# The order of gate and branch tiles in the tail of a hybrid decoder layer

## The chip, the cores and the metric

The kernel runs on one core of a Trainium2 chip. The metric is the device time of one execution in microseconds (us); where several runs are shown, their median counts.

## The reference, cut to what matters

One layer is computed in float32 for 512 prompt tokens and 8 sample tokens. The normalised and modulated input `h` goes through one projection `w_in`, whose columns feed two recurrent branches, their gates, and two merge gates `ga` and `gb`:

```
mod = silu(c) @ w_mod + b_mod                 # six parts: shift, scale and gate, twice
u = h @ w_in                                  # qa, fa, ia, oga, xb, yb, ga, gb
o_a = rmsnorm(hgrn2(...)) * silu(oga)         # eight heads
o_b = rglru(...) * gelu(yb)
merged = sigmoid(ga) * (o_a @ w_branch_a) + sigmoid(gb) * (o_b @ w_branch_b)
x = x + g1 * (merged @ w_out)
h2 = rmsnorm(x) * (1 + sc2) + sh2
x = x + g2 * (square(relu(h2 @ w_ff1)) @ w_ff2)
y = rmsnorm(x)
```

The final states of the recurrences and of the convolution are outputs too.

## The kernel before, in words

**Tiling.** Activations lie transposed, 128 features on the partitions and T = 520 tokens along the free axis, as two halves of 260. Every factor of a large product is split into a rounded part and the rest (`hi`, `lo`), and `products` (L144) makes hi*hi, hi*lo and lo*hi of it. So one output tile of 128 features over an inner length of 1024 (`gemm`, L156) is 8 x 3 x 2 = 48 matmuls. Such a tile is the unit of work below: a gate tile, a branch tile, an output projection tile.

**Weights.** `weights`, `take_w` and `ready_w` (L85 to L142) hand them out in the order of the steps. A 512 KB tile of weights is loaded on SP's queue (`_load_w`, L97) into one of four staging buffers `wst`, LOADS = 3 ahead of the splitting; ACT writes `whi` (L112), DVE `wlo` (L115), AHEAD = 2 tiles before use, into one of two places. The rows of `w_mod` need no splitting: they go through the same four buffers and are read there by PE.

**Modulation.** `mod` (L438) is one modulation step: two row tiles of 512 KB, on each of which `mod_rows` (L410) issues four matmuls (two records each in the trace, so 16 a step, L413). Four steps make a part; ACT then copies its sums (L418), and `mod_cols` (L421, matmuls of L427) turns them within the next gemm. Four parts are left for the tail, so 16 steps. `mod_step` in `run` puts one after a tile.

**Order of the steps.** `run` (L1555) writes a list of steps, each with its weights, and then calls them. First come eight heads, with the RG-LRU columns between them. Heads are finished two at a time (`heads_prompt`, L636), so that the end of heads 6 and 7 lies under the gate tiles that follow. `head_prompt` (L707) ends with: transposes (L714), states (L720), outputs (L731 and L733, into `pt`), their mean square (L738) and scale (L743) on ACT, transposes back (L747), the product with the output gate on DVE (L749), and a store to DRAM on SP's queue (L750). `heads_sample_done` (L626, L632) and `heads_sample_out` (L752, L758) close the sample tokens.

Then comes the tail:

- eight gate tiles b (`gate`, L891: gemm on `h`, then a sigmoid on ACT, L175, into a slot of pool `ma`). After the fourth, at TAIL = 3, `end_recurrences` and `begin_tail` (L1829) stand;
- eight branch tiles b (`branch`, L897: gemm on `ob`, then DVE multiplies the gate by it, L899). `rg_out` (L859) stands after the second: PE transposes of the last states (L871), copies (L873) and stores on POOL's queue (L875);
- eight times a gate tile a (into a slot of pool `tail`) and a branch tile a (`merge`, L901: gemm on `oa`, product, sum of both branches, split of the result);
- `load_xT` (L917: the residual's input, transposes of L933), `shifts` (L939: two memsets of the new `h` on POOL, L945), `begin_strassen` (L1840), then eight output projection tiles, which read all eight merged tiles.

`begin_tail` closes the pools of the recurrences (`rg`, `hg`) and opens those of the tail on their memory; a tile there waits for the tiles that it lies over. `load_branches` (L879) loads `ob` (L883) and `oa` (L887) back from DRAM on POOL's queue through five slots `t`; ACT and DVE split them (L205, L206).

**What sets the order on an engine.** The framework's scheduler places the instructions of neighbouring steps among each other on every engine; each engine then runs its own list in order. The list of steps is thus close to PE's order, but not the same. Only the beginning of the kernel (`begin`, L1635) is kept in order by hand; its instructions are recorded through a helper and show as L69. It ends with `again`, which puts the first modulation's shift into `h` (ACT into the rounded part, DVE through `ht` into the rest), with the pools `rg` and `hg` and with POOL's memsets of `fkq` and `at` (L1810). The first head's f, q and g products are made there; its v product (in `pt` and `pb`) is the first gemm behind.

Of the kernel before, what the change touches and what calls it, by code (L numbers as in the profile page):

```python
# [6 lines left out]
F32 = mybir.dt.float32  # L7
# [11 lines left out]
T = L + NB  # L19
HALF = T // 2  # L20
KO = D // 128
# [3 lines left out]
DFF = 4 * D  # L25
EPS = 1e-6
AHEAD = 2
TAIL = 3
URGENT = 200
TOGETHER = 400  # L30
NWM = 8
# [45 lines left out]
class Kernel:  # L77
# [1477 lines left out]
    def run(self):  # L1555
        tc, i, enter = self.tc, self.i, self.ctx.enter_context
        self.consts = enter(tc.tile_pool(name="consts", bufs=1))
        self.dram = enter(tc.tile_pool(name="dram", bufs=1, space=DRAM))
        self.sm = enter(tc.tile_pool(name="sm", bufs=2))
        self.wst = enter(tc.tile_pool(name="wst", bufs=WST))  # L1560
        self.ma = enter(tc.tile_pool(name="ma", bufs=8))
        self.ppt = enter(tc.tile_pool(name="ppt", bufs=1, space=PSUM))
        self.ppb = enter(tc.tile_pool(name="ppb", bufs=1, space=PSUM))
        self.pmm = enter(tc.tile_pool(name="pmm", bufs=2, space=PSUM))
        self.pps = enter(tc.tile_pool(name="pps", bufs=2, space=PSUM))
        self.whl = enter(tc.tile_pool(name="whl", bufs=2))
        self.act = enter(tc.tile_pool(name="act", bufs=2))
        self.early = ExitStack()
        self.hc = self.early.enter_context(tc.tile_pool(name="hc", bufs=1))
        self.ogs = self.hc.tile([128, H, NB], F32, name="ogs")  # L1570
        self.os = self.hc.tile([128, H, NB], F32, name="os")
        self.xlast = self.hc.tile([128, KO, 11], F32, name="xlast")
        self.hlast = self.hc.tile([128, KO, 9], F32, name="hlast")
        self.oaT_d = self.dram.tile([H, 128, L], F32, name="oaT_d")
        self.obT_d = self.dram.tile([KO, 128, T], F32, name="obT_d")
        self.oa, self.ob, self.merged = [], [], []

        win = i["w_in"][0]
        steps = []
        one = lambda name, m, fn, *a: steps.append(([(i[name][0], 0, m * 128)], fn, *a))  # L1580
        mods = [(p, k) for p in (2, 4, 3, 5) for k in range(0, KO, 2)]

        def mod_step():
            p, k = mods.pop(0)
            steps.append(([self.mod_key(p, k + n) for n in range(2)], self.mod, p, k))

        ga, gb = {}, {}
        self.rg = {}

        for h in range(H):  # L1590
            kf, kq, kv, kg = self.head_cols(h)
            steps.append(([kf, kq, kg, kv][FIRSTS if h == 0 else 0:], self.head_start if h == 0 else self.head, h))
            for n in (h - 1, h) if h % 2 else (h, h + 1):
                one("w_in", (40 if h % 2 else 32) + n, self.rg_y if h % 2 else self.rg_x, n)
        for m in range(KO):
            one("w_in", 56 + m, lambda m: gb.update({m: self.gate(7, m, self.slot(self.ma, "ma"))}), m)
            if m == TAIL:
                steps.append(([], self.end_recurrences))
                steps.append(([], self.begin_tail))
            if m > TAIL and m % 2:  # L1600
                mod_step()
        for m in range(KO):
            if m == 2:
                steps.append(([], self.rg_out))
            one("w_branch_b", m, lambda m: self.branch("w_branch_b", m, self.ob, gb[m]), m)
            if m <= TAIL or m % 2:
                mod_step()
        for m in range(KO):
            one("w_in", 48 + m, lambda m: ga.update({m: self.gate(6, m, self.slot(self.tail, "t"))}), m)
            one("w_branch_a", m, lambda m: self.merge(m, ga.pop(m), gb.pop(m)), m)  # L1610
            mod_step()
        steps.append(([], self.load_xT))
        steps.append(([], self.shifts))
        steps.append(([], self.begin_strassen))
        for m in range(KO):
            one("w_out", m, self.out_proj, m)
        steps.append(([], self.norm2))
        self.entries, self.use = self.plan()
        steps.append((self.entries[:FIRST], self.mlp))

        keys = [k for st in steps for k in st[0]]
        self.mlp_at = len(keys) - FIRST
        self.weights(keys)
        self.begin()
        for _, fn, *a in steps:
            fn(*a)
# [8 lines left out]
    def begin(self):  # L1635
# [167 lines left out]
        self.rgp = self.open_pool("rg", 2, reuse_waits="tile")  # L1803
        self.hg = self.scope.enter_context(self.tc.tile_pool(name="hg", bufs=2, reuse_waits="tile"))
        self.opened = {}
        self.X = [self.hg.tile([128, 3, T], F32, name=f"X{n}", bufs=1) for n in range(4)]
        self.fkq = [self.hg.tile([128, 3, 32], F32, name=f"fkq{n}", bufs=1) for n in range(4)]
        self.at = self.hg.tile([128, 2, NC, C], F32, name="at", bufs=1)
        for t in (*self.fkq, self.at):
# [19 lines left out]
    def begin_tail(self):  # L1829
        self.close_pool()  # L1830
        tc = self.tc
        pool = lambda name, bufs, **kw: tc.tile_pool(name=name, bufs=bufs, reuse_waits="tile", **kw)
        self.misc = self.ctx.enter_context(pool("misc", 1, side="right"))
        self.right = ExitStack()
        self.abb = self.right.enter_context(pool("abb", 16, side="right"))
        self.tail = self.open_pool("tail", 2, reuse_waits="tile")
        self.ab = self.scope.enter_context(pool("ab", 16))
        self.load_branches()

    def begin_strassen(self):  # L1840
        self.right.close()
        self.sw = self.ctx.enter_context(self.tc.tile_pool(name="sw", bufs=2, side="right", reuse_waits="tile"))


# [32 lines left out]
```

## Time and profile before

| | |
|---|---|
| three runs | 1031.09, 1031.99, 1032.07 us; median 1031.99 |
| the profiled execution | 1030.22 us |
| its span, first to last instruction | 1028.4 us |
| mean granted TensorE clock | 0.995 |
| PE, DVE, ACT, POOL busy | 97%, 66%, 50%, 12% of the span |

A row of the timeline reads: start in us, duration in us, engine, line, operation, output<-inputs, shapes, how many in a row, and in brackets the idle time ahead of it with what ended it. A row of a group has, after the bar, busy us and the mean ns of one, then the idle time ahead. A row of the DMA issues has the count, the size of each, and the median us from issue to landing. PE's matmuls overlap, so the step from one start to the next counts, not the duration of one. Lines named Lnnn are those of the kernel before; of after, those above L1580 are a few lines further down.

### The profile page before, as it was taken

The page shows a single profiled execution, that of the slowest core. Times are in us where ns is not written, and L with a number is a line of the kernel's source. Part 1 is how long each engine was busy: PE and PEld are TensorE (multiplying, and loading weights), DVE is VectorE, ACT ScalarE, POOL GpSimd, SP SyncE. Part 2 cuts the span into 40 slices and gives each one's busy share as a digit, 9 for nine tenths or more (in the row PEclk, how much of TensorE's full clock was granted, in tenths as well). Part 3 has the DMA queues.
Part 4 walks back from the last instruction along what each step waited for, and adds up shares of the span by engine and source line. Part 5 has one row for each costly group of instructions (what it writes and reads, how often), then busy time and mean ns, then how long its engine had stood idle before and what let it go on. Part 6 is the DMA issues. An engine that isn't in the chain of part 4 may idle for free. (4 is left out here: it accounts for less than half of the span.)

```text
span 1028.4 us, 23561 instructions
## 1 busy us (share of the span) xinstructions
PE 997.9 (97%) x9756; PEld 965.4 (94%) x9756; DVE 678.3 (66%) x1428; ACT 513.9 (50%) x964; POOL 123.8 (12%) x229
## 2 busy tenths in 40 slices
PE   5999999999999999989999999999999999999997
PEld 2899899999999999969999999999999999999997
DVE  7785868687586858355233347677776776777685
ACT  4555644644564554342122235466556655656663
POOL 3210000000000001011000001011421231232150
PEclk9999999999999999999999999999999999999998
DMA  9663353444334445268555568322672484274242
GB/s 324 222 201 111 95 160 101 133 134 134 101 103 149 116 124 156 89 230 264 167 157 173 162 179 240 97 83 62 134 180 78 93 177 121 52 157 101 63 83 83
DMA packets 201822, 143.67 MB, mean 140 GB/s; under 512 B 6767, under 2 KB 189703, under 8 KB 201707
## 3 DMA queue, kind: packets, MB, share of 16 engines
q1 hardware_dynamic: 191090, 128.08, 41.5%
q0 software_dynamic: 10608, 14.05, 7.1%
q8 instruction: 76, 1.25, 0.5%
q14 instruction: 32, 0.25, 0.1%
q10 hardware_dynamic: 16, 0.03, 0.0%
HBM read 123.61 MB, written 11.26 MB: 131 GB/s over the span
## 5 line engine op out<-in xcount | busy, mean ns | idle before, releaser
L151 PE MATMUL mm<-h,whi 128*128 128x260 f32 (+1 forms) x2944 | 489.2, 285 | 0.0
L151 PEld LDWEIGHTS mm<-h,whi 128*128 128x128 f32 x2944 | 409.1, 188 | 4.5 <-ACT whi L112 3.3
L151 PE MATMUL mm<-h,wlo 128*128 128x260 f32 x1472 | 302.0, 284 | 0.0
L115 DVE TENSOR_TENSOR wlo<-wst,whi 128x1024 fp32r<-128x1024 f32 x164 | 200.1, 1221 | 124.8 <-ACT whi L112 123.2
L112 ACT CAST whi<-wst 128x1024 fp32r<-128x1024 f32 x164 | 171.8, 1049 | 214.5 <-PE mm L151 180.5
L151 PEld LDWEIGHTS mm<-h,wlo 128*128 128x128 f32 x1472 | 230.0, 189 | 0.4 <-issue 0.2
L151 PE MATMUL mm<-a,whi 128*128 128x260 f32 x512 | 84.3, 285 | 0.0
L151 PEld LDWEIGHTS mm<-a,whi 128*128 128x128 f32 x512 | 70.4, 188 | 2.5 <-issue 2.1
L151 PE MATMUL mm<-a,wlo 128*128 128x260 f32 x256 | 52.3, 284 | 0.0
L883 POOL DMA_DIRECT2D t<-obT_d x8 | 4.4, 552 | 386.8 <-PE pb L788 311.5
L1276 DVE TENSOR_TENSOR f<-f 128x260 f32<-128x260 f32 x64 | 27.3, 427 | 27.6 <-ACT f L1271 26.9
L1265 ACT ACTIVATE ft<-ft,fsh 128x512 f32<-128x512 f32 (+2 forms) x36 | 24.0, 675 | 36.1 <-DVE ft L1262 36.1
L151 PE MATMUL mm<-b,whi 128*128 128x260 f32 x256 | 41.1, 282 | 0.0
L1268 POOL TENSOR_TENSOR ft<-ft,fsh 128x8 f32<-128x8 f32 x28 | 18.5, 659 | 186.7 <-DVE ft L1262 146.5
L151 PEld LDWEIGHTS mm<-a,wlo 128*128 128x128 f32 x256 | 39.6, 188 | 0.0
L151 PEld LDWEIGHTS mm<-b,whi 128*128 128x128 f32 x256 | 35.0, 188 | 0.0
L1310 POOL DMA_DIRECT2D ma<-snap x28 | 27.7, 1002 | 35.0 <-issue 26.2
L681 DVE TENSOR_TENSOR X<-X,tb 128x512 f32<-128x512 f32 x48 | 31.8, 682 | 0.0
L1292 POOL DMA_DIRECT2D ma<-snap x28 | 25.9, 927 | 41.1 <-DMA ma<-snap 29.3
L1271 ACT ACTIVATE f<-ft 128x520 f32<-128x520 f32 (+1 forms) x36 | 20.8, 587 | 15.1 <-POOL ft L1269 13.0
L597 DVE SCALAR_TENSOR_TENSOR st<-vb,fkq,st 128x128 f32<-128x128 f32 x64 | 17.5, 345 | 14.6 <-DMA vb<-vd 14.6
L151 PE MATMUL mm<-b,wlo 128*128 128x260 f32 x128 | 25.9, 284 | 0.0
(571 smaller groups left out, 1871.3 us busy)
## 6 DMA issues: line engine op xcount, KB each, us to landing
wst<-in_w_in_dram SPq DMA_DIRECT2D x64, 512.0 KB, 4.2
wst<-in_w_mod_dram SPq DMA_DIRECT2D x32, 512.0 KB, 4.6
wst<-in_w_ff_dram SPq DMA_DIRECT2D x64, 256.0 KB, 3.6
wst<-in_w_ff_dram SPq DMA_DIRECT2D x32, 512.0 KB, 4.9
wm<-in_w_mod_dram SPq DMA_DIRECT2D x16, 512.0 KB, 10.5
st<-in_state_hgrn_dram SPq DMA_DIRECT2D x8, 512.0 KB, 5.2
vb<-vd SPq DMA_DIRECT2D x8, 512.0 KB, 3.4
out_dram<-st SPq DMA_DIRECT2D x8, 512.0 KB
```

The lines of the kernel that those rows point to most:

```text
L112: ins = self.nc.scalar.copy(hi, st)
L115: self.nc.vector.tensor_tensor(lo, st, hi.bitcast(F32), OP.subtract)
L151: self.last_product = self.nc.tensor.matmul(ps[s][:, :c.stop - c.start], x, y[:, c], start=first and n == 0, stop=last and n == 2)
L597: nc.vector.scalar_tensor_tensor(st[:, b], vb[:, b], fkq[:, 1, b:b + 1], st[:, b], OP.mult, OP.add)
L681: nc.vector.tensor_tensor(half, half, fac, OP.mult)
L883: nc.gpsimd.dma_start(t, self.obT_d[n])
L1265: nc.scalar.activation(t[:, :p], t[:, :p], AF.Relu, bias=sh[:, 0:1])
L1268: eng.tensor_tensor(t[:, p:], t[:, p:], sh[:, 1:9], OP.add)
L1271: nc.scalar.activation(f, self.two(self.ft)[:, a:a + n], AF.Square)
L1276: self.nc.vector.tensor_tensor(f[:, n], f[:, a], f[:, b], op)
L1292: nc.gpsimd.dma_start(x[1][:, b], v[:, :n], accum_op=OP.add)
L1310: nc.gpsimd.dma_start(x[t][:, a], s[p], accum_op=OP.add)
```

## The change

All eight gate tiles b and then all eight gate tiles a come first; branch b's eight tiles follow, then branch a's eight. TAIL goes from 3 to 6, so `begin_tail` stands after the seventh gate tile b. Gate a's results get a pool `gp` of eight tiles on the right side of the memory, where `misc` was; `misc` is opened in `begin_strassen` only, when `gp` and `abb` are closed. The 16 modulation steps are spread evenly over the 25 tiles behind `begin_tail`. Of the four tiles `X`, the first two move to a pool `hx` of their own, above `hg`.

```diff
-TAIL = 3
+TAIL = 6
...
-        def mod_step():
+        def mod_step(due):
+            if due < 0.999 or not mods:
+                return due
             p, k = mods.pop(0)
             steps.append(([self.mod_key(p, k + n) for n in range(2)], self.mod, p, k))
+            return due - 1
...
-        for m in range(KO):
-            one("w_in", 56 + m, lambda m: gb.update({m: self.gate(7, m, self.slot(self.ma, "ma"))}), m)
-            if m == TAIL:
+        tiles = [("b", m) for m in range(KO)] + [("a", m) for m in range(KO)]
+        share, due = len(mods) / (2 * len(tiles) - TAIL - 1), 0.0
+        for g, m in tiles:
+            if g == "b":
+                one("w_in", 56 + m, lambda m: gb.update({m: self.gate(7, m, self.slot(self.ma, "ma"))}), m)
+            else:
+                one("w_in", 48 + m, lambda m: ga.update({m: self.gate(6, m, self.slot(self.gp, "gp"))}), m)
+            if (g, m) == ("b", TAIL):
                 steps.append(([], self.end_recurrences))
                 steps.append(([], self.begin_tail))
-            if m > TAIL and m % 2:
-                mod_step()
-        for m in range(KO):
-            if m == 2:
+            if (g, m) > ("b", TAIL) or g == "a":
+                due = mod_step(due + share)
+        for g, m in tiles:
+            if (g, m) == ("b", 2):
                 steps.append(([], self.rg_out))
-            one("w_branch_b", m, lambda m: self.branch("w_branch_b", m, self.ob, gb[m]), m)
-            if m <= TAIL or m % 2:
-                mod_step()
-        for m in range(KO):
-            one("w_in", 48 + m, lambda m: ga.update({m: self.gate(6, m, self.slot(self.tail, "t"))}), m)
-            one("w_branch_a", m, lambda m: self.merge(m, ga.pop(m), gb.pop(m)), m)
-            mod_step()
+            if g == "b":
+                one("w_branch_b", m, lambda m: self.branch("w_branch_b", m, self.ob, gb[m]), m)
+            else:
+                one("w_branch_a", m, lambda m: self.merge(m, ga.pop(m), gb.pop(m)), m)
+            due = mod_step(due + share)
+        assert not mods, mods
...
-        self.X = [self.hg.tile([128, 3, T], F32, name=f"X{n}", bufs=1) for n in range(4)]
+        hx = self.scope.enter_context(self.tc.tile_pool(name="hx", bufs=1, reuse_waits="tile"))
+        self.X = [(self.hg if n > 1 else hx).tile([128, 3, T], F32, name=f"X{n}", bufs=1) for n in range(4)]
...
-        self.misc = self.ctx.enter_context(pool("misc", 1, side="right"))
         self.right = ExitStack()
+        self.gp = self.right.enter_context(pool("gp", 8, side="right"))
         self.abb = self.right.enter_context(pool("abb", 16, side="right"))
...
     def begin_strassen(self):
         self.right.close()
+        self.misc = self.ctx.enter_context(self.tc.tile_pool(name="misc", bufs=1, side="right", reuse_waits="tile"))
         self.sw = self.ctx.enter_context(self.tc.tile_pool(name="sw", bufs=2, side="right", reuse_waits="tile"))
```

## The prediction

> **What bounds the kernel now.** I read the page's busy times first, then the table of 20 us stretches, then PE's instructions in order of time in the one stretch that is not full, and last the queues that feed it.
>
> ```profile
> PE 997.9 (97%) x9756; PEld 965.4 (94%) x9756; DVE 678.3 (66%) x1428; ACT 513.9 (50%) x964; POOL 123.8 (12%) x229
> ```
>
> ```profile
> 420.00:440.00 20.00, 20.00 (x171) 20.00 (x170) 6.13 (x12) 7.14 (x19) 0.00 (x0) 1.00 0.39 122
> 440.00:460.00 20.00, 15.24 (x120) 10.31 (x119) 11.90 (x41) 7.68 (x16) 4.33 (x8) 0.91 0.64 216
> 460.00:480.00 20.00, 20.00 (x184) 18.40 (x183) 13.77 (x23) 7.80 (x12) 3.70 (x7) 1.00 0.88 279
> 480.00:500.00 20.00, 20.00 (x181) 18.55 (x180) 5.78 (x6) 3.15 (x3) 0.52 (x1) 1.00 0.67 200
> ```
>
> PE is the bound: 97% of the span, and full before and after the seam between recurrences and tail. Columns of the stretches: length, then busy us of PE, PEld, DVE, ACT and POOL, granted clock, DMA share, GB/s. The change can only win what PE loses at the seam, 440 to 460: 4.76 us idle, and a granted clock of 0.91.
>
> ```profile
> 438.08 0.49 PE L151 MATMUL mm<-h,whi 128*128 128x260 f32 x2
> ...
> 441.29 0.40 PE L151 MATMUL mm<-h,wlo 128*128 128x260 f32 x2
> 443.42 0.66 PE L747 MATMUL pt<-ident,g 128*128 128x128 f32 x4 [1.73 <-ACT g L743]
> 444.86 0.65 PE L632 MATMUL pt<-ident,sev 128*128 128x128 f32 x4 [0.79 <-DVE e L749]
> 445.78 3.48 PE L413 MATMUL pt<-wst,cT 128*32 128x256 f32 x30 [0.27 <-DVE os L634]
> 449.18 0.43 PE L758 MATMUL ps<-sq,ones_r 128*128 128x64 f32 x2
> 449.55 0.62 PE L413 MATMUL pt<-wst,cT 128*32 128x256 f32 x2
> ...
> 456.06 0.62 PE L413 MATMUL pt<-wst,cT 128*32 128x256 f32 x2 [1.98 <-DMA wst<-in_w_mod_dram]
> ...
> 470.65 0.60 PE L871 MATMUL ps<-ident,hlast 128*9 128x128 f32 x4
> 471.00 0.36 PE L151 MATMUL mm<-a,wlo 128*128 128x260 f32 x1
> ...
> 474.52 0.53 PE L427 MATMUL pb<-ident,modev 128*128 128x36 f32 x4
> 474.98 1.07 PE L413 MATMUL pt<-wst,cT 128*32 128x256 f32 x16
> ...
> 481.93 1.07 PE L413 MATMUL pt<-wst,cT 128*32 128x256 f32 x16
> ...
> 494.62 1.07 PE L413 MATMUL pt<-wst,cT 128*32 128x256 f32 x16
> ```
>
> ```profile
> 444.00:446.00 2.00, 0.95 (x9) 0.62 (x12) 0.87 (x2) 0.24 (x2) 0.00 (x0) 0.89 0.16 63
> 446.00:448.00 2.00, 2.00 (x24) 0.88 (x19) 1.44 (x3) 2.00 (x5) 0.45 (x1) 0.50 0.22 78
> ```
>
> At 441.53 (two matmuls after 441.29, at 0.12 each) the last gate tile is done. Everything left needs either the end of head 7 (L747, L632) or branch b's operand, which comes after it. PE does the modulation rows it has (L413) at a granted clock down to 0.50, starts branch b, and waits 1.98 for the next rows.
>
> ```profile
> 436.49 0.33 SPq L101 DMA_DIRECT2D wst<-in_w_mod_dram  x1
> 444.83 0.33 SPq L750 DMA_DIRECT2D oaT_d<-e  x1
> 446.92 0.38 SPq L103 DMA_DIRECT2D wst<-in_w_branch_b_dram  x1
> 447.77 0.82 SPq L101 DMA_DIRECT2D wst<-in_w_mod_dram  x1
> ...
> 447.56 1.76 POOL L883 DMA_DIRECT2D t<-obT_d  x3 [52.59 <-DVE a L206]
> ```
>
> SP's own order makes it worse: the store of head 7's result (L750) stands ahead of branch b's weights, so nothing was issued on it for 8 us, and then weights, rows and branch operands are fetched at once.
>
> **The change, part by part.** The built program of after, compared engine by engine, has the same instructions as before on every engine; only places between some 441 and 630 us differ, and some waits.
>
> (1) *Gates first.* How much does the seam cost? From 441.53 to the sixth modulation step at 481.93 are 40.40 us. In them PE does four branch tiles of 48 matmuls, five modulation steps, 24 transposes, one L427 and one L758. A tile with a step is 481.93 - 474.98 = 6.95; two tiles with a step are 494.62 - 481.93 = 12.69; so a tile is 5.74 and a step 1.21. Four transposes are 471.00 - 470.65 = 0.35, so 24 are 2.1; L427 is 474.98 - 474.52 = 0.46; L758 is 449.55 - 449.18 = 0.37. Work: 4 x 6.95 + 1.21 + 2.1 + 0.46 + 0.37 = 31.94. **Lost at the seam: 40.40 - 31.94 = 8.46 us**: the idle 4.76, the rest slow clock and refilled pipeline.
>
> ```profile
> L112 ACT CAST whi<-wst 128x1024 fp32r<-128x1024 f32 x164 | 171.8, 1049 | 214.5 <-PE mm L151 180.5
> ...
> wst<-in_w_mod_dram SPq DMA_DIRECT2D x32, 512.0 KB, 4.6
> ```
>
> ```profile
> t<-oaT_d POOLq DMA_DIRECT2D x8, 256.0 KB, 6.7
> t<-obT_d POOLq DMA_DIRECT2D x3, 260.0 KB, 8.0
> ```
>
> In after, eight gate tiles a, which need only h, stand at that place. On PE's list, behind head 7's last state product (ahead of 438.08), come 69 gate matmuls, L747, 27 more, L632, 22 more, the first rows and L758, then gates to the end. At 0.12 us a matmul (5.74 / 48) L747 is reached at 438.08 + 8.3 = 446.4. In before its operand was there at 443.42; ACT now has one weight copy ahead of it (L112, 1.05 us by its group), which makes 444.5. So no wait. Branch b starts some 50 us later (eight gates at 5.74 and steps), when its operands have long been split: in before they were all there within the first branch tile. All 8.46 can go.
>
> What is late next? Rows and weights. The four staging buffers go round in turn: a step's second row tile is issued when the step before has read its first, and is needed one tile and one step later, 5.74 + 1.21 = 6.95 us. The median landing of the 32 is 4.6. In the crowded seam rows issued at 447.77 were there at 456.06: 8.3 us, 1.3 too many. After has 11 loads of branch operands (8 x 256 and 3 x 260 KB, which took 6.7 and 8.0 us to land between 430 and 500) beside its first two or three steps, as before had. The leftover is bounded by nothing and two waits like 456.06's (2 x 1.98 = 4.0). I take 0.4, nearest to nothing: before ran 460 to 480 at a DMA share of 0.88 with PE full.
>
> A rule that speaks against this part: the Trainium skill ("DMA: Bandwidth & Descriptors", Queues, rings and completion order) says that each DMA engine serves the queues with work in turn, packet by packet. By it SP's weights would get half while POOL's loads run: no trace here shows the split, and the sum by it would be about 2 us worse, one such wait.
>
> (2) *Modulation steps spread evenly.* 16 steps as before, on 25 places. Eight of the 15 distances are one tile long, in before two. They cost nothing while rows land within 6.95 us; the price if not is a rival below.
>
> (3) *Pool gp, TAIL 6, rg_out, shifts.* Gate a's sigmoid writes gp, which lies over X0 and X1 (last used by heads 4 and 5): its only wait in the built program is PE's. Eight results held until the merge cost no engine time. POOL's two memsets of h (L945) move ahead of the state outputs (L875) and wait for the last gate, which PE has done before L871: nothing queues. The merge of the last branch a (three operations of DVE and one of ACT, on half L112's columns, so under 4 x 1.05 = 4.2 us) is hidden by the first seven eighths of an output projection tile, 7/8 x 5.74 = 5.0; without that cover it costs 4.2 at most. ACT and DVE have room: under 14 of 20 us busy from 440 to 500. misc, opened later, is first written when the last merge has read gp.
>
> (4) *X0 and X1 in pool hx.* This moves addresses at the head of the kernel, which the diff does not show. In before POOL's memsets (L1810) had nothing to wait for; in after they wait for the last ht on DVE.
>
> ```profile
> 53.07 0.54 DVE L69 TENSOR_SCALAR ht<-xn,modT,shp 128x512 f32<-128x512 f32 x1
> ...
> 53.98 0.68 DVE L69 TENSOR_TENSOR h<-ht,h 128x512 fp32r<-128x512 f32 x1
> 54.59 1.79 DVE L69 TENSOR_SCALAR ht<-xn,modT,shp 128x512 f32<-128x512 f32 x1
> ...
> 53.74 0.99 POOL L1673 TENSOR_TENSOR h<-fs,h 128x8 fp32r<-128x8 f32 x1
> 54.67 0.53 POOL L1810 MEMSET fkq<- 128x96 f32 x4
> 55.13 0.96 POOL L1810 MEMSET at<- 128x1024 f32 x1
> ...
> 57.88 0.28 PE L151 MATMUL pb<-h,whi 128*128 128x260 f32 x1
> 58.16 0.39 PE L151 MATMUL pt<-h,whi 128*128 128x260 f32 x1
> ...
> 58.86 0.28 PE L151 MATMUL pb<-h,whi 128*128 128x260 f32 x1
> 59.41 0.39 PE L151 MATMUL pt<-h,whi 128*128 128x260 f32 x1 [0.28 <-DVE h L69]
> ```
>
> Beside the memsets one ht took 1.79 instead of 0.54, 1.25 more, and PE then stood 0.16 and 0.43 us over its 0.12 at 58.16 and 59.41. Without that delay both stalls go: **0.6**. At worst the memsets, later now, hit the last subtraction in its place, and the gain is 0; DVE's subtraction at 53.98 beside a POOL operation took its usual 0.68, so I take 0.6. The Trainium skill ("SBUF — State Buffer", Who interferes with whom) says that a two-input DVE operation collides with GpSimd reads, not with pure writes: by it too 0.6. The read at 53.74 did not slow 53.98 either, which the rule would have had. The first sigmoid into X0 waits for PE's last shift product instead of for DVE's last ht, which comes later, so it holds up nobody.
>
> **Sum.** 8.46 - 0.4 + 0.6 = 8.66 us. On the profiled execution, 1030.22 (span 1028.4 and 1.8 around it), that is 1021.6; the median of the runs shown is 1031.99, 1.77 above, so **1023.4 us** predicted. The bounds: at best 9.1 (1022.9), at worst 8.46 - 4.0 = 4.5 (1027.5).
>
> **The rivals.** (A) *The seam's DMA crowd stays*, chance 0.15: POOL's operand loads now run beside gates that need weights as well, and rows come late once or twice. For it: 8.3 us against 6.95. Against it: SP now has weights up to gate a 3 issued ahead of head 7's store, and the loads have eight tiles' time instead of one. The rule above (the Trainium skill, "DMA: Bandwidth & Descriptors") would lead here. Gain 5 to 6.5: 1025.5 to 1027.
>
> (B) *The even spread starves PE*, slower, 0.04: in all eight short distances the second row tile lands after 8.3 us instead of 4.6. Each costs 1.35, together 10.8, against a gain of 8.46: 2.3 slower, 1034.3. It decides from 8.46 / 8 = 1.06 us each, a landing of 8.0. Against it: outside the seam DMA's share of 480 to 500 is 0.67, and before had such a distance from 474.98 to 481.93 with PE full.
>
> (C) *Nothing comes of it*, 0.03: the seam's slack is given back where something else is timed by DMA or by the chain of heads, so 1031.5. Against it: PE is full from 460 on.
>
> (D) The forecast with its 0.4 and 0.6, 0.78: 1022.3 to 1025.5 with the spread of runs.
>
> **How the numbers follow.** 1023.4 is D's. D and nearly all of A hold the time 9 in 10; cutting A's top, the range for 8 in 10 is 1022.3 to 1026.6. Faster than 0.2% (2.1 us, about what a measurement tells from no change) are D and A: 0.93; C makes 0.03 the same; B 0.04 slower.
>
> **What would show it.** Right: 440 to 460 with PE at 20.00 and clock 1.00; no wait at L747 and L632; the ht by 54.59 at 0.54; the whole span from the first rows to the first L933 shorter by some 8. Wrong: waits of PE for row tiles behind gates a 2 and a 3 (A), or at every second tile up to the output projection (B); a new wait of PE near 120 or 200 us (C).

## The result, and the profile after

After: **1024.07 us**, median of four runs (1022.04 to 1024.82); before beside it 1031.54 (1029.1 to 1032.07). The ratio is 0.9929, with a 95% interval of 0.9907 to 0.9951, so the change gains 0.7%: 7.5 us between the medians, and by the interval 5.1 to 9.6. The profiled execution of after is the slowest of its four, 1024.82 us with a span of 1023.0.

The page's busy times of after, then its stretches of 20 us (length, busy us of PE, PEld, DVE, ACT and POOL with their instructions, granted clock, DMA share, GB/s):

```profile
PE 998.3 (98%) x9756; PEld 969.0 (95%) x9756; DVE 676.8 (66%) x1428; ACT 512.7 (50%) x964; POOL 123.6 (12%) x229
```

```profile
420.00:440.00 20.00, 20.00 (x171) 20.00 (x170) 7.66 (x14) 6.24 (x11) 0.00 (x0) 1.00 0.31 96
440.00:460.00 20.00, 20.00 (x174) 18.97 (x173) 10.97 (x31) 10.57 (x26) 3.25 (x6) 1.00 0.49 146
460.00:480.00 20.00, 20.00 (x181) 18.56 (x180) 12.64 (x30) 10.07 (x16) 2.69 (x5) 1.00 0.97 328
480.00:500.00 20.00, 20.00 (x182) 18.65 (x181) 3.89 (x5) 4.91 (x7) 0.23 (x2) 1.00 0.63 186
```

PE's busy time is what it was; the span is shorter. In 440 to 460, PE has gone from 15.24 busy at a clock of 0.91 to 20.00 at 1.00. The DMAs are most crowded in 460 to 480, as in before (0.97 against 0.88), and PE stays full beside them.

PE's timeline of after at the seam, and SP's queue there. A bracket at the end of a row would be idle time ahead of it; PE's rows have none:

```profile
440.43 0.39 PE L733 MATMUL pt<-g,X 128*128 128x128 f32 x2
...
448.92 0.60 PE L747 MATMUL pt<-ident,g 128*128 128x128 f32 x4
...
452.60 0.60 PE L632 MATMUL pt<-ident,sev 128*128 128x128 f32 x4
...
455.78 0.64 PE L413 MATMUL pt<-wst,cT 128*32 128x256 f32 x8
456.35 0.43 PE L758 MATMUL ps<-sq,ones_r 128*128 128x64 f32 x2
```

```profile
439.00 7.69 SPq L103 DMA_DIRECT2D wst<-in_w_in_dram  x2
450.28 0.34 SPq L750 DMA_DIRECT2D oaT_d<-e  x1
452.50 4.30 SPq L101 DMA_DIRECT2D wst<-in_w_mod_dram  x2
```

In before, PE came to the end of head 7 (L747, L632) with nothing else to do, and then read 30 records' worth of rows in one lump. Here the gates' matmuls stand between these rows, the first lump of rows is 8, and SP has issued two weight tiles of the gates (L103) ahead of the store L750, where before had one row tile.

To see where the time came from, I cut each profiled execution at four instructions of PE: the first v product (the first gemm, L151), the last L733 (the end of head 7 begins), the first L933 (behind the tail), the end. In us:

| | start of the span to v product | to the last L733 | **tail**: to the first L933 | to the end | span |
|---|---|---|---|---|---|
| before | 53.45 | 384.60 | **172.90** | 417.49 | 1028.43 |
| after | 56.30 | 384.24 | **165.01** | 417.49 | 1023.04 |

The tail gained 7.89. The last stretch is the same to a hundredth. At the start, which the change doesn't touch, this execution of after lost 2.85, beside a lower granted clock. These are the 20 to 40 us of before and then of after:

```profile
20.00:40.00 20.00, 18.30 (x180) 14.68 (x179) 14.16 (x33) 10.15 (x16) 0.87 (x3) 1.00 0.97 336
```

```profile
20.00:40.00 20.00, 18.56 (x145) 15.86 (x146) 13.16 (x27) 10.14 (x16) 0.87 (x3) 0.83 0.94 327
```

The clock was 0.83 instead of 1.00, and PE did 145 matmuls instead of 180 in those 20 us. The starts of all 14 profiled kernels go by this clock and not by kernel: eight at 1.00 took 53.42 to 53.69, two at 0.91 took 53.92 and 54.02, four at 0.83 took 55.46 to 56.30. One execution of 1024.82 therefore says little by itself, and the experiments below are compared by the tail. The tail repeats well: e8 and e12, the same kernel, both took 164.76.

### The profile page after: what moved, and what is told of

Read it like the earlier page. It is cut to its first block, busy times and chain, and to the rows that moved or that the text cites. A ratio compares the mean times of both kernels' runs of the same rounds, so it can differ in the third digit from the quotient of the medians.

```text
span 1023.0 us, 23553 instructions
## 1 busy us (share of the span) xinstructions
PE 998.3 (98%) x9756; PEld 969.0 (95%) x9756; DVE 676.8 (66%) x1428; ACT 512.7 (50%) x964; POOL 123.6 (12%) x229
## 5 line engine op out<-in xcount | busy, mean ns | idle before, releaser
L151 PE MATMUL mm<-h,whi 128*128 128x260 f32 (+1 forms) x2944 | 490.4, 286 | 0.0
L151 PEld LDWEIGHTS mm<-h,whi 128*128 128x128 f32 x2944 | 410.2, 189 | 3.3 <-issue 1.8
L151 PE MATMUL mm<-h,wlo 128*128 128x260 f32 x1472 | 302.9, 285 | 0.3 <-DVE wlo L115 0.3
L151 PEld LDWEIGHTS mm<-h,wlo 128*128 128x128 f32 x1472 | 230.9, 189 | 1.1 <-DVE wlo L115 0.5
L151 PE MATMUL mm<-a,whi 128*128 128x260 f32 x512 | 84.0, 284 | 0.0
L151 PEld LDWEIGHTS mm<-a,whi 128*128 128x128 f32 x512 | 70.3, 188 | 1.7 <-ACT whi L112 1.6
L151 PE MATMUL mm<-a,wlo 128*128 128x260 f32 x256 | 52.3, 284 | 0.0
L151 PE MATMUL mm<-b,whi 128*128 128x260 f32 x256 | 41.6, 285 | 0.0
L151 PEld LDWEIGHTS mm<-a,wlo 128*128 128x128 f32 x256 | 39.6, 188 | 0.0
L151 PEld LDWEIGHTS mm<-b,whi 128*128 128x128 f32 x256 | 35.1, 188 | 2.1 <-ACT whi L112 1.2
L151 PE MATMUL mm<-b,wlo 128*128 128x260 f32 x128 | 25.9, 283 | 0.0
```

The source lines that it names most:

```text
L151: self.last_product = self.nc.tensor.matmul(ps[s][:, :c.stop - c.start], x, y[:, c], start=first and n == 0, stop=last and n == 2)
```

## The experiments

Each experiment has one profiled execution, and one of them was timed in further runs as well. In the table, "idle" is PE's idle time in the tail, and "rest" runs from the last L733 to the end. The rest is needed for the three kernels with dense steps (e7, e9, e10): their last column transposes (four matmuls of L427 and eight transposes of L924) come before the first L933 instead of behind it, some 1.1 us that move from the last stretch into the tail. In the other kernels that last stretch took 417.38 to 418.24, so differences in the rest of under 0.9 us say little.

| | what it is | tail | rest | idle | that run |
|---|---|---|---|---|---|
| before | | 172.90 | 590.39 | 4.76 | 1030.22 |
| after | | 165.01 | 582.50 | 0.00 | 1024.82 |
| e1 | after, no gate a ahead of branch b | 172.46 | 590.63 | 3.62 | 1030.49 |
| e5 | after, one gate a ahead | 168.13 | 586.30 | 0.98 | 1024.95 |
| e6 | after, two gates a ahead | 166.05 | 583.78 | 0.04 | 1022.44 |
| e2 | before with pool hx | 172.83 | 591.08 | 3.51 | 1030.62 |
| e3 | after without pool hx | 165.12 | 582.51 | 0.00 | 1024.88 |
| e4 | before, head 7's store on POOL | 173.81 | 591.32 | 5.67 | 1030.50 |
| e7 | after, a step behind every tile | 175.13 | 591.42 | 4.33 | 1032.50 |
| e9 | e7, operand loads late | 170.52 | 586.90 | 2.60 | 1028.65 |
| e10 | a step behind every tile from gate a 2 | 165.85 | 582.21 | 0.00 | 1025.72 |
| e8 | after, steps behind branch tiles only | 164.76 | 582.60 | 0.00 | 1020.92 |
| e11 | after with TAIL = 3 | 171.93 | 589.61 | 4.01 | 1028.67 |
| e12 | e8 again, timed | 164.76 | 582.42 | 0.00 | 1022.64 |

### Is it the order of the tiles, and how many does it take? (e1, e5, e6)

Theory: PE lacks work at the seam, so the gain goes by the work put there. e1 is after with its eight gates a back in front of their branch tiles; e5 and e6 leave one or two of them ahead.

```diff
-        for g, m in tiles:                  # the gates
+        for g, m in tiles[:KO + N]:         # N = 0, 1, 2
...
             else:
+                if m >= N:
+                    one("w_in", 48 + m, lambda m: ga.update({m: self.gate(6, m, self.slot(self.gp, "gp"))}), m)
+                    due = mod_step(due + share)
                 one("w_branch_a", m, lambda m: self.merge(m, ga.pop(m), gb.pop(m)), m)
```

> After with everything but the order of the tiles: gate tiles a stand again in turn with branch tiles a, while TAIL 6, the even spread of the steps, pools gp and hx stay. 'The tail' is the time from head 7's last state product (last L733) to the first transposes of the residual's input (first L933): 172.90 us in before, 165.01 in after. Theory of the prediction (only gate tiles that need nothing of the heads cover the seam): the tail stays at 172 to 174, PE idles 4 to 6 us between 440 and 460, one execution about 1030 to 1032. Rival (the even spread of the steps and the later begin_tail made the gain): 165 to 167.

> After with only the first gate tile a ahead of branch b; the other seven stand each before its branch tile a, as before had all eight. The tail is the span from the last L733 to the first L933: 172.90 us before, 165.01 after, 172.46 with no gate tile a ahead. Theory (the gain is work that PE can do while head 7 ends and branch b's operands come, so it goes by the amount): one tile covers 48 x 0.12 = 5.74 us of the lost 8.46, so the tail is 165.0 + 2.7 = 167.7 (166.5 to 169). Rival (it's SP's order and the crowd of loads, so a single tile helps little, because branch b's weights still stand behind head 7's store): 170 to 172. Rival (any tile is enough): 165.

> After with two of the gate tiles a ahead of branch b, the other six as before. Theory (by the amount): two tiles are 11.5 us of work, more than the lost 8.46, so nothing is left to gain: tail 165.0 to 166. Rival (crowd of loads: rows and operands are fetched at once, and only eight tiles' time spreads them): two or three late rows of 1.3 to 2 us each, 168 to 171.

Measured: 172.46, 168.13 and 166.05, against 165.01 with eight. Above the seam's work of 172.90 - 8.46 = 164.44, that is 8.0, 3.7, 1.6 and 0.6 us. The first tile is worth 4.3 and the second 2.1; all of the other six together 1.0. The theory holds with its sizes, but for two small misses: e6 is 0.05 above its range, and e1's idle time was 3.62 where 4 to 6 was expected. "Any tile is enough" falls, as does "a single tile helps little". PE's waits at the seam in e1, and then in e5:

```profile
444.14 1.12 PE L747 MATMUL pt<-ident,g 128*128 128x128 f32 x4 [2.43 <-ACT g L743]
446.04 1.12 PE L632 MATMUL pt<-ident,sev 128*128 128x128 f32 x4 [0.79 <-DVE e L749]
447.42 1.93 PE L413 MATMUL pt<-wst,cT 128*32 128x256 f32 x16 [0.27 <-DVE os L634]
```

```profile
447.55 1.07 PE L413 MATMUL pt<-wst,cT 128*32 128x256 f32 x16 [0.27 <-DVE os L634]
...
467.64 0.74 PE L151 MATMUL mm<-a,whi 128*128 128x260 f32 x4 [0.71 <-ACT whi L112]
```

In e1 the waits of before are back, and behind them the slow clock: four transposes last 1.12 us instead of 0.60, and 16 records of L413 1.93 instead of 1.07. The idle 3.62 is under half of the 8.0 lost. Most of the rest is this clock: it averaged 0.51 from 444 to 451, which makes some 3.4 us (an estimate, 7 x 0.49). In e5 the waits for g and e are gone and the clock holds at 1.00. Only 0.98 of the 3.7 us that e5 still loses is idle time; the rest is in steps of PE that are longer than usual, most of them from 462 to 468, and was not taken apart.

### Does the placement of X0 and X1 do anything? (e2, e3)

e2 is before with pool hx and nothing else of the change; e3 is after without it.

```diff
+        hx = self.scope.enter_context(self.tc.tile_pool(name="hx", bufs=1, reuse_waits="tile"))
-        self.X = [self.hg.tile([128, 3, T], F32, name=f"X{n}", bufs=1) for n in range(4)]
+        self.X = [(self.hg if n > 1 else hx).tile([128, 3, T], F32, name=f"X{n}", bufs=1) for n in range(4)]
```

> Before with pool hx alone. Theory: only the head of the kernel changes. POOL's memsets wait for the last ht on DVE, the ht that took 1.79 us takes 0.54, PE's two short stalls in the first gemm go, and the stretch from the first gemm (first L151) to head 7's last state product (384.60 us in before, 384.24 in after) is 384.2; the tail stays at 172.9. Rival (the 0.4 of that stretch comes from elsewhere): 384.6.

> After with all four X back in pool hg, so that gp lies over other tiles of the recurrences. Theory (the order makes the gain, placement makes none): the tail is 165.0 within 0.5, the stretch ahead of it 384.6. Rival (gp has to lie over X0 and X1): the first sigmoids of gate a wait for tiles that head 7 still uses, its store included, ACT stands and PE with it, and the tail is 167 or more.

The long stretch to the last L733 can't tell: 384.34 and 385.02, where after had 384.24 and before 384.60, and the other experiments between 382.86 and 386.25. Its first part can. From the v product to the first L632, the three kernels without hx (before, e3, e4) took 134.59, 134.54 and 134.56. Seven with hx (e1, e2, e5, e6, e8, e11, e12) took 133.74 to 133.76. That is **0.8 us**, to a few hundredths in every kernel. Compared matmul by matmul from the v product on, e12 is ahead of before by 0.25 at the 40th and by 0.79 at the 46th, and that difference stays, within 0.05, to the 1200th: it arises just where before's two stalls lay. (The other four kernels with hx, after among them, took 135.27 or 135.28. They lost 1.5 us further on, at a slow clock; see the end.) DVE, POOL and PE of e2 there:

```profile
54.57 0.54 DVE L69 TENSOR_SCALAR ht<-xn,modT,shp 128x512 f32<-128x512 f32 x1
...
58.35 0.53 DVE L587 COPY fkq<-ma 128x8 f32<-128x8 f32 x1
```

```profile
57.43 0.53 POOL L1811 MEMSET fkq<- 128x96 f32 x4 [2.72 <-DVE ht L69]
57.88 0.98 POOL L1811 MEMSET at<- 128x1024 f32 x1
```

```profile
57.98 0.28 PE L151 MATMUL pt<-h,whi 128*128 128x260 f32 x1
58.10 0.28 PE L151 MATMUL pb<-h,whi 128*128 128x260 f32 x1
58.22 0.28 PE L151 MATMUL pt<-h,wlo 128*128 128x260 f32 x1
```

The memsets now start behind the last ht; the ht at 54.57 takes 0.54 and not 1.79, and PE goes on in steps of 0.12. What the memset hits instead is a small copy, 0.53 where the same copy takes 0.16 without it, and DVE's next operation starts 0.12 behind its start all the same. This is that copy in before, where the memsets were over by then:

```profile
59.61 0.16 DVE L587 COPY fkq<-ma 128x8 f32<-128x8 f32 x1
```

The tail has no need of hx: 165.12 without it. So the theory holds for both kernels, and e3's rival, that gp has to lie over X0 and X1, falls.

### Was it the store on SP's queue? (e4)

The prediction said that SP's order made before's seam worse: head 7's store L750 stood ahead of branch b's weights. e4 is before with that one store on POOL's queue.

```diff
-        nc.sync.dma_start(self.oaT_d[h], oa[:, :L])
+        (nc.gpsimd if h == H - 1 else nc.sync).dma_start(self.oaT_d[h], oa[:, :L])
```

> Before with the store of head 7's result (L750) issued on POOL's queue instead of SP's, so that no weights stand behind it. Theory (the seam lacks work that needs no head; the queue only adds the one wait of 1.98): the tail goes from 172.9 to 170.9 at best. Rival (SP's order is what makes the seam): the tail falls by 4 or more, to 169 or less.

Measured: 173.81, no gain. The reason is in the list of SP's waits (queue and line, what it waited for, us in total, times, longest), first of before and then of e4, in 436 to 460:

```profile
SPq L750 <- DVE e L749: 7.9, 1, 7.9
```

```profile
SPq L103 <- PE pt L413: 12.1, 2, 9.6
```

With the store gone, the weight behind it waits just as long, for PE to read rows: all four staging buffers were full (PE then reads 32 records of L413, which are four row tiles). **The store hid the real wait.** The 0.9 by which e4 is longer than before is idle time (5.67 against 4.76), nearly all of it one wait of 0.81 for a split operand, which before doesn't have; why that operand came late was not followed up. e1 shows the same from the other side. There the scheduler put branch b's weights ahead of the store, and the seam still lost 8.0:

```profile
436.53 7.68 SPq L103 DMA_DIRECT2D wst<-in_w_branch_b_dram  x2
446.01 0.34 SPq L750 DMA_DIRECT2D oaT_d<-e  x1
```

### Do short distances between steps cost anything? (e7, e8)

e7 puts a step behind every tile from the seventh gate b on; e8 puts none among the gates, and one behind each of the 16 branch tiles. In the list of steps both have 15 distances of one tile, where after, on PE, has eight.

```diff
-        share, due = len(mods) / (2 * len(tiles) - TAIL - 1), 0.0
+        share, due = 1, 0.0
```

and in e8 also

```diff
-            if (g, m) > ("b", TAIL) or g == "a":
-                due = mod_step(due + share)
```

> After with a modulation step behind every tile from the seventh gate tile b on until all 16 are used, so that all 15 distances are one tile long and the first nine lie beside the loads of the branch operands. Theory of the prediction (rows land within a tile and a step, 6.95 us, but for some in the crowd): tail 165 to 167. Rival A (rows are late in the crowd, 1.3 to 2.0 us each for three to five of them): 168 to 172. Rival B (every short distance costs 1.35 us, seven more of them than after has): 165.0 + 9.5 = 174.5.

> After with no modulation step among the gate tiles: one behind each of the 16 branch tiles, so all 15 distances are one tile long, but none lies beside the loads of the branch operands. Theory of the prediction (short distances cost nothing outside the crowd): tail 164.4 to 165.2, with the 0.57 us that after still loses gone or not. Rival B (a short distance costs 1.35 us wherever it is): 165.0 + 9.5 = 174.5.

e7's 175.13 is close to the number of rival B, and all of the gain is gone. But e8 has as many short distances and stands at 164.76, and e7's loss isn't spread over 15 places. It lies in one. PE, SP and ACT of e7:

```profile
459.10 0.61 PE L871 MATMUL ps<-ident,hlast 128*9 128x128 f32 x4 [0.34 <-DVE rows L873]
463.70 1.23 PE L151 MATMUL mm<-h,whi 128*128 128x260 f32 x4 [4.00 <-ACT whi L112]
464.73 1.05 PE L871 MATMUL ps<-ident,hlast 128*9 128x128 f32 x4
465.71 1.08 PE L413 MATMUL pt<-wst,cT 128*32 128x256 f32 x8
```

```profile
437.75 7.64 SPq L101 DMA_DIRECT2D wst<-in_w_mod_dram  x2
449.03 0.33 SPq L750 DMA_DIRECT2D oaT_d<-e  x1
455.23 0.38 SPq L103 DMA_DIRECT2D wst<-in_w_in_dram  x1
```

```profile
462.60 1.04 ACT L112 CAST whi<-wst 128x1024 fp32r<-128x1024 f32 x1 [4.07 <-DMA wst<-in_w_in_dram]
```

SP's list of waits in 440 to 460 of e7 names what kept the weight back until 455.23:

```profile
SPq L103 <- PE ps L758: 6.1, 1, 6.1
```

Two steps' rows sit in the staging buffers, and PE reads them only around the sample tokens' end (L632, L758). Until then no weight can be fetched for the gates that should fill the seam. The weight comes 7.4 us after its issue, PE stands 4.00, and the next 6 us run at a slow clock (four matmuls of L871 take 1.05 instead of 0.61; PE's steps are normal again from 469.93 on). So B has nearly the right number and the wrong mechanism; rival A's price is real, but it isn't paid in after.

### Full buffers or crowded DMAs? (e9, e10)

e9 is e7 with the operand loads held back behind gate a 4; e10 starts the dense steps at gate a 2, so that no rows stand ahead of L758, with the loads where they were.

```diff
+            nc.vector.tensor_copy(t[:, :8], after[:, :8])
             nc.gpsimd.dma_start(t, self.obT_d[n])
...
+            if (g, m) == ("a", 4):
+                steps.append(([], lambda: self.load_branches(ga[4])))
...
-        self.load_branches()
```

This is e9; the loads of `oaT_d` get the same copy. In e10:

```diff
-            if (g, m) > ("b", TAIL) or g == "a":
+            if g == "a" and m >= 2:
                 due = mod_step(due + share)
```

Both have e7's `share = 1` as well.

> The kernel with a step behind every tile (e7) once more, but each load of a branch operand on POOL's queue waits for gate tile a 4 (a copy of eight columns of its result into the buffer that the load then overwrites), so that no operand load lies beside the first steps. In e7 the loss lay at one place: SP stood 6.1 us at a weight whose staging buffer held a row tile that PE reads behind L758, issued it at 455.23, the copy L112 ran at 462.60, and PE waited 4.00 and was slow behind it; tail 175.13. Theory ring (the four staging buffers are full of rows that PE can't read yet): the issue stays late, the landing is a quiet one of 4.2 instead of 7.4 us, the wait is still some 1 us or more, the tail 168 to 172. Theory crowd (only the operand loads make it late): no wait, tail 164.5 to 167. If the tail stays at 174 to 176, it's neither.

> After with a step behind every tile from gate tile a 2 on until all 16 are used: no rows are taken ahead of L758, but the distances are all one tile, and the operand loads still lie beside the first gates a. Theory ring: nothing holds the staging buffers over the end of head 7, tail 164.4 to 165.5. Theory crowd: rows and weights are late beside the loads too, tail 166 to 170. Rival B of the prediction (each short distance costs 1.35): 174.5.

e9: 170.52, in the range of the ring theory. Its PE row with the wait, its SP row and its copy:

```profile
463.02 0.74 PE L151 MATMUL mm<-h,whi 128*128 128x260 f32 x4 [2.26 <-ACT whi L112]
```

```profile
456.78 0.38 SPq L103 DMA_DIRECT2D wst<-in_w_in_dram  x1
```

```profile
461.92 1.04 ACT L112 CAST whi<-wst 128x1024 fp32r<-128x1024 f32 x1 [2.34 <-DMA wst<-in_w_in_dram]
```

The weight is issued as late as in e7, with none of POOL's operand loads beside it, and is there after 5.1 us instead of 7.4 (4.2 was expected). The wait is 2.26 instead of 4.00. In the rest, e9 loses 4.4 us on after and e7 8.9. e10: a tail of 165.85, between the two ranges that were set; some 1.1 of it are the column transposes that moved in. Its rest is 582.21, as good as after (582.50), and PE has no wait in it although the loads lie beside it. So the full buffers decide. The crowd alone costs nothing here, but it adds 2.3 us of landing once they have made a weight late, and the loss is then twice that of e9.

### Does it need TAIL = 6? (e11)

```diff
-TAIL = 6
+TAIL = 3
```

> After with TAIL at 3 as before had it: the pools are closed, and the first step stands, behind the fourth gate tile b and not the seventh; the steps are spread over 28 places. The prediction's part 3 (where the pools close costs nothing, all that opens there waits for head 7 anyhow): tail 164.4 to 166. Rival (steps three tiles sooner fill the staging buffers while head 7 still ends, as in e7): 168 to 175.

Measured: 171.93. The prediction's part 3 falls, and its rival holds. With all gates in the order of after, 6.9 of the 7.9 us are lost again. PE and SP of e11:

```profile
447.80 1.93 PE L413 MATMUL pt<-wst,cT 128*32 128x256 f32 x32 [0.27 <-DVE os L634]
...
453.73 0.74 PE L151 MATMUL mm<-h,whi 128*128 128x260 f32 x4 [1.52 <-ACT whi L112]
...
457.88 1.08 PE L413 MATMUL pt<-wst,cT 128*32 128x256 f32 x8 [1.18 <-DMA wst<-in_w_mod_dram]
```

```profile
435.73 0.33 SPq L101 DMA_DIRECT2D wst<-in_w_mod_dram  x1
446.52 0.33 SPq L750 DMA_DIRECT2D oaT_d<-e  x1
448.50 1.00 SPq L103 DMA_DIRECT2D wst<-in_w_in_dram  x2
```

It is before's picture: two steps' rows (x32, before x30) are read in one lump at the sample tokens' end. They are four row tiles and fill all four staging buffers, so SP issues the next weights only then, at 448.50. The gates a are there to fill the seam, but their weights are not. TAIL sets both where the pools close and where the first step stands; e7 shows that early steps alone do this. Whether closing the pools early costs anything besides was not tried.

### The shortest tail, timed (e12)

> The kernel of e8 again, timed: all 16 steps behind the branch tiles. Its tail was 164.76, 0.25 under after's, so if nothing else counts it gains 8.1 to 8.5 us on before: a ratio of 0.991 to 0.993, with after's 0.9929 inside its interval. If the one run of 1020.92 was typical, 0.9895 or less.

Median 1022.80 of six runs (1020.55 to 1024.46), beside 1031.77 of eleven of before: a ratio of 0.9911, interval 0.9892 to 0.9929. It is faster than before. The ratio lies in the 0.991 to 0.993 expected, though the gain, 9.0 us, is above the 8.1 to 8.5 that went with it; e8's one run of 1020.92 was not typical. Than after (0.9929) it is at most a little faster: the intervals overlap, and the tails differ by 0.25 us.

## Why the prediction was right, point by point

**The sum.** Forecast 1023.4, measured 1024.07. Of the terms, the tail was to gain 8.06 (8.46 less 0.4) and gained 7.89; the head was to gain 0.6 and gained 0.8. Together that is 8.7 of the 8.66 forecast; that the two misses cancel is luck. The medians lie only 7.5 apart; the missing 1.2 is inside the interval of 5.1 to 9.6 and can't be told from the spread of the runs.

**(1) Gates first: right in size and place.** The leftover was 0.57 (165.01 - 164.44) against 0.4 forecast. L747 came 8.4 us after the last L733 (the second of the two at 440.43, at 440.54; 448.92 - 440.54), forecast 8.3, and without a wait. The late rows that the leftover was for were not seen: PE has no wait there. A weight was late, though. This is ACT's copy in after:

```profile
466.77 1.05 ACT L112 CAST whi<-wst 128x1024 fp32r<-128x1024 f32 x1 [3.66 <-DMA wst<-in_w_in_dram]
```

SP had issued it at 457.41, 9.4 us before. ACT waited 3.66 for it, and PE didn't, since copies run two tiles ahead. The Trainium skill ("DMA: Bandwidth & Descriptors", Queues, rings and completion order) had SP's transfers share each DMA engine with POOL's. The 7.4 against 5.1 us of e7 and e9 agrees with it in direction; the split itself no run here shows. By that rule one wait of 2 us was to come in after, and none did.

**One reason ahead of (1) was wrong:** "the store of head 7's result (L750) stands ahead of branch b's weights, so nothing was issued on it for 8 us". e4 took the store away and the weight waited on, for staging buffers full of rows.

**(2) The even spread: right.** e8 and e10 have 15 short distances, and their rest is that of after within 0.3 us. Rival B falls.

**(1) and (3), who earns the gain: this is the step that failed.** (3) names TAIL 6 and gives it no effect, and e11's expectation says of it "where the pools close costs nothing". As a cost it is nothing, but it was no bystander. The prediction gave all 8.46 to the order of the tiles. e11 shows that the order without TAIL 6 gains 1.0 of it, e1 that TAIL and the spread without the order gain 0.4. The gain needs both: work that doesn't hang on head 7, and staging buffers that are free to fetch its weights. The sum came out right because the built list that it was read from held both, so it did not have to know which of them pays. Gate a's pool, the memsets of h and the merge cost nothing: the stretch from the first L933 is 417.49 in both.

**(4) Pool hx: right mechanism, 0.8 instead of 0.6.** Behind each of the two long steps the next one was long too (58.16 to 58.38 and 59.41 to 59.64, 0.22 and 0.23 instead of 0.12), and the forecast left those out.

**Rivals.** A's late transfers exist (e7, e9, and the weight above), but in after they fall on slack. C falls: nothing was given back.

## What to carry to other kernels

A seam where one chain ends and the next begins is closed by work that hangs on neither, and one or two tiles of it do most; but that work's own loads must get through, so look at what holds the staging buffers over the seam before you move tiles. When a queue stands at one instruction, ask what the next one behind it would wait for: taking the first away may only show the second. And when two edits come together, undo each by itself before you say which one pays.

## What the runs showed of the hardware that was not expected

**Short gaps were followed by a slower clock.** In after, PE waits twice for 0.67 us around 129 us, with 19 matmuls between. These are those waits, and the 4 us behind them:

```profile
128.75 0.45 PE L669 MATMUL ps<-X 128*32 128x32 f32 x16 [0.67 <-DVE X L681]
...
130.42 0.45 PE L669 MATMUL ps<-X 128*32 128x32 f32 x16 [0.67 <-DVE X L681]
```

```profile
130.00:134.00 4.00, 3.58 (x32) 3.54 (x33) 3.93 (x14) 2.69 (x5) 0.00 (x0) 0.65 0.56 176
```

The granted clock averaged 0.65 over them and 1.5 us were lost. In e8 the same two waits (0.63 and 0.67) left the clock at 1.00. All 14 profiled executions have these two waits, and up to there the same instructions in the same order on each engine. Four had the drop and ten had not, so it goes by execution and not by kernel, and the waits alone don't decide it. The Trainium skill ("TensorE: Matmul & The Clock Gate", Why this matters for your kernels) advises against idle gaps of over some 3 us; here it came behind gaps of 0.67, and of 1.73 with 0.79 in before.

**A memset on POOL slows some of DVE's operations.** A one-input operation beside it took 1.79 instead of 0.54, or 0.53 instead of 0.16; a two-input one beside it took its usual 0.69 (in after, at 60.32):

```profile
60.32 0.69 DVE L69 TENSOR_TENSOR h<-ht,h 128x512 fp32r<-128x512 f32 x1
```

The Trainium skill ("SBUF — State Buffer", Who interferes with whom) says that copies and tensor_scalar can take the port that DVE shares with GpSimd and then block for a whole instruction, and that a two-input operation minds GpSimd's reads only. Both agree with these rows. The prediction set a POOL operation that reads, at 53.74 in before, against the second rule, because DVE's 53.98 beside it was not slowed. That POOL operation took 0.99 itself, where others on the same line and of the same shape took as little as 0.20, so it may have been the one held up, and the row speaks neither for nor against.
